# Delta layer: sixteen broadcast transfers issued from ScalarE's queue instead of SyncE's

## The chip, the cores and the metric

The kernel runs on one core of one Trainium2 chip. The metric is the device time of one execution in microseconds (us), median of three runs. Engines are named as the profile names them: PE (TensorE), DVE (VectorE), ACT (ScalarE), POOL (GpSimd), SP (SyncE, here only a queue from which transfers are issued).

## What is computed

One inference step of a two-layer decoder trunk, for 512 prompt positions and 8 sample rows together (520 columns), model width 1024. Layer 0 mixes tokens by causal pooling, layer 1 by a gated delta rule with 8 heads of 128; a gated feed-forward layer follows each. The part that the change touches is the delta rule, cut to what matters:

```python
gc = jnp.cumsum(g, axis=-1)                                   # log decay within a chunk
decay = jnp.exp(jnp.where(incl, gc[..., :, None] - gc[..., None, :], -jnp.inf))
a_mat = jnp.where(strict, einsum('id,jd->ij', kb, k) * decay, 0.0) + eye
rhs = jnp.concatenate([vb, kb * jnp.exp(gc)[..., None]], axis=-1)
sol = triangular_solve(a_mat, rhs, lower=True, unit_diagonal=True)
qk = einsum('id,jd->ij', q, k) * decay
q_dec = q * jnp.exp(gc)[..., None]
# then a scan over the chunks with the state S
```

The kernel uses four chunks of 128 positions a head (the result is the same for any chunk length). For `decay` it needs, for each head, `gc` of the chunk's positions as a row that is the same on all 128 partitions; for `q_dec` it needs `exp(gc)` in the same form. Both are made by writing a 32x128 tile to DRAM (`gdr` for gc, `edr` for exp(gc)) and reading it back with every partition getting the same row.

## The kernel before, in words

All arrays are feature-major: 128 partitions hold features, the free axis holds the 520 columns. Every dense product is done as three fp32r matmuls (high times high, high times low, low times high part). The weights stream through as chunks of 128x1024 (512 KB): SP issues the load of `wr` (two buffers), ACT casts it to `wh`, DVE subtracts to get `wl` (class `Weights`, lines 312 to 368). A new load is issued only when `wl` has been made from the buffer that it overwrites (`adv_lo`, line 351).

The delta layer's input product runs tile by tile (32 tiles of 128 output features; each takes two halves of 24 matmuls on PE). Around it, for each of eight heads, a set of small tasks is put in between: `t_em` (decay of a pair of heads, line 1136), `t_head` (transposes, norms, products of keys and queries, line 1151), `t_v`, `t_leaf` and `levels` (triangular inverse, on POOL and PE), `t_scan` and `t_out` (state scan), `t_norm`, `t_split`, and `t_sample` for the sample rows.

The order is made when the program is built. A planner (`Clock`, `Engine`, `Background`, lines 48 to 309) keeps an expected time for each engine and for each buffer, and lays down a task's next instructions when the expected time of PE has reached the time at which their inputs are expected. Each engine then executes its own list strictly in the order in which it was laid down, whatever the real times are; PE too. So an instruction laid down too early makes its engine stand, with all that is behind it. For a transfer the planner expects this (lines 166 to 172):

```python
if op == "dma_start":
    t = max([self.c.at.get(name, 0.0), self.c.dma[0]] + [...ready...])
    self.c.dma[0] = t + 0.48
    self.c.dma[1] = max(t + 1.1, self.c.dma[1]) + 4 * outs[0].shape[0] * n / 3.6e5
    self.c.at[name] = t
    cost = 0.06
    extra = self.c.dma[1] + 0.9 - t
```

`name` is the issuing engine, so `self.c.at[name] = t` sets the expected time of that engine to the time of the issue. With both inputs ready and no earlier transfer under way, a 128x512 tile is expected 1.1 + 0.73 + 0.9 = 2.73 us after its issue.

The two transfers in question:

- `em[h]` <- `gdr` (line 1142, in `t_em`): 128x512 f32, 256 KB, for both heads of a pair one after the other. DVE then makes four pieces per head (`em<-em,lg,msk`, line 1146), ACT the exponential (line 1133), and DVE uses it in `U` (line 1194) and in `em<-em,pk` (line 1197).
- `vn[h]` <- `edr` (line 1181, in `t_head`): the same size, one per head. DVE multiplies the queries with it (`kq<-kq,vn`, line 1202). That buffer later holds the values (`t_v`, line 1219), so the tile has two uses.

Eight of each: 16 transfers, 4 MB. Besides these SP issues all weight loads, the small stores of states, and the spills. ACT issues eight loads of `in_ssm` (line 1474) in the delta layer.

The sample task of a pair (`t_sample`, line 1466) makes two small products on DVE (`s_sq`, `s_pr`, lines 1482 and 1483) and lays a small PE matmul group behind them (`p_q<-ones,s_sq`, line 1486).

In the text, em(h) and vn(h) are the transfers of head h, counted from 0.

Of the kernel before, what the change touches and what calls it, by code (L numbers as in the profile page):

```python
# [22 lines left out]
NH, NCH = 8, 4  # L23
# [363 lines left out]
def _emit(tc, nc, clk, E, P, a, o):  # L387
    V, S, G, PE, SP = (E[k] for k in ("DVE", "ACT", "POOL", "PE", "SP"))
# [20 lines left out]
    def aux(name="aux"):  # L409
        k = min((k for k in banks if banks[k] is None), key=bank_at)  # L410
        banks[k] = (psd["p"] if k == "r3" else psa).tile([128, 512], F32, name, tag=k, bufs=1)[:]
        return banks[k]

    def give(p):
        k, = (k for k in banks if banks[k] is p)
        banks[k] = None
# [534 lines left out]
    def delta_in(res, dp, oz, oz1, r8):  # L951
# [11 lines left out]
        gdr = dram.tile([32, 128], F32, "gdr")  # L963
        edr = dram.tile([32, 128], F32, "edr")
# [45 lines left out]
        def t_ab():  # L1010
# [60 lines left out]
            SP.dma_start(out=gdr, in_=gcT)  # L1071
            flags.add("gc")
            bg.add(t_em(0), 0)
            yield [lg[:]], "ACT", None
            S.activation(out=eg, in_=lg, func=AF.Exp)
# [35 lines left out]
        em, kq, U, kd, vn, vt, v, vf = {}, {}, {}, {}, {}, {}, {}, {}  # L1111
# [7 lines left out]
        def alloc(kind, shape=(128, NCH, 128)):  # L1119
            return dp.tile(list(shape), F32, kind, bufs=bufs[kind])  # L1120

        def take(kind, n=1):
            assert free[kind] >= n
            free[kind] -= n
# [5 lines left out]
        def em_exp(hh):  # L1130
            act_table("exp_and_others")
            for h in hh:
                S.activation(out=em[h], in_=em[h], func=AF.Exp)
                done["em"].add(h)

        def t_em(pair):
            hh = (2 * pair, 2 * pair + 1)
            yield [gdr[:], lambda: dp.free_at("em", bufs["em"])], None, both(lambda: "gc" in flags, can("em", 2))
            take("em", 2)
            for h in hh:  # L1140
                em[h] = alloc("em")
                SP.dma_start(out=em[h], in_=gdr[:].rearrange("(c h) i -> h c i", h=8)[h].unsqueeze(0).broadcast_to([128, NCH, 128]))
            for h in hh:
                for c in range(NCH):
                    yield [em[h][:]] if c == 0 else [], "DVE", None
                    V.scalar_tensor_tensor(out=em[h][:, c, :], in0=em[h][:, c, :], scalar=gcl[:, 0, hc(c, h)], in1=msk,
                                           op0=ALU.subtract, op1=ALU.min)
            yield [em[hh[1]][:]], "ACT", lambda: "ln" in flags
            em_exp(hh)

        def t_head(h):
            yield [], None, both(is_done("kq", h), can("kd"), lambda: "eg" in flags)
            take("kd")
            for i in (0, 1):
                yield [kq[h][:, i, :], aux_free], None, aux_ok
                pt = aux("pt")
                for c in range(NCH):
                    PE.transpose(pt[:, tok[c]], kq[h][:, i, tok[c]], ident)
                n2 = dp.tile([128, NCH], F32, "n2", bufs=4)
                if i == 0:  # L1160
                    kd[h] = alloc("kd")
                for c in range(NCH):
                    yield [pt[:, tok[c]]], "ACT", None
                    jk = dp.tile([128, 128], F32, "jk")
                    S.activation(out=jk, in_=pt[:, tok[c]], func=AF.Square, accum_out=n2[:, c:c + 1])
                    if i == 0:
                        S.activation(out=kd[h][:, c, :], in_=pt[:, tok[c]], func=AF.Copy, scale=ekd[:, hc(c, h)])
                give(pt)
                yield [n2[:]], "DVE", None
                if i == 0:  # L1170
                    V.tensor_scalar(out=n2, in0=n2, scalar1=EPS, scalar2=None, op0=ALU.add)
                    bg.add(t_nk(h, n2), 2)
                    r = dp.tile([128, NCH], F32, "n2r", bufs=2)
                    V.reciprocal(out=r, in_=n2)
                    V.tensor_tensor(out=sc_s[:, h, :], in0=r, in1=beta[:, 0:4, h], op=ALU.mult)
                else:
                    V.tensor_scalar(out=epsq[:, h, :], in0=n2, scalar1=EPS, scalar2=EPS * 128.0, op0=ALU.add, op1=ALU.mult)
            yield [edr[:]], None, both(lambda: "er" in flags, can("vn"))
            take("vn")
            vn[h] = alloc("vn")  # L1180
            SP.dma_start(out=vn[h], in_=edr[:].rearrange("(c h) i -> h c i", h=8)[h].unsqueeze(0).broadcast_to([128, NCH, 128]))
            yield [], None, both(is_done("em", h), can("U"))
            take("U")
            U[h] = alloc("U")
            for c2 in range(2):
                yield [kq[h][:], aux_free], None, aux_ok
                pk = aux("pk")
                for q in range(2):
                    c = 2 * c2 + q
                    PE.matmul(pk[:, q * 256:q * 256 + 256], kq[h][:, 0, tok[c]], kq[h][:, :, tok[c]], start=True, stop=True)  # L1190
                for q in range(2):
                    c = 2 * c2 + q
                    yield [pk[:, q * 256:q * 256 + 256], em[h][:, c, :], sc_s[:, h, :]], "DVE", None
                    V.scalar_tensor_tensor(out=U[h][:, c, :], in0=pk[:, q * 256:q * 256 + 128], scalar=sc_s[:, h, c:c + 1],
                                           in1=em[h][:, c, :], op0=ALU.mult, op1=ALU.mult)
                yield [], "DVE", None
                V.tensor_tensor(out=em[h][:, 2 * c2:2 * c2 + 2, :], in0=em[h][:, 2 * c2:2 * c2 + 2, :],
                                in1=pk[:].rearrange("p (q x) -> p q x", q=2)[:, :, 128:], op=ALU.mult)
                give(pk)

            yield [vn[h][:]], "DVE", None
            V.tensor_tensor(out=kq[h][:, 1, 0:T], in0=kq[h][:, 1, 0:T], in1=vn[h][:].rearrange("p c x -> p (c x)"), op=ALU.mult)
            done["head"].add(h)

        def t_nk(h, n2):
            yield [n2[:]], "POOL", None
            G.tensor_tensor(out=nk[:, h, :], in0=n2, in1=half[:, 0:NCH], op=ALU.pow)
            done["nk"].add(h)
# [436 lines left out]
        for pair in range(NH // 2):  # L1645
            hh = (2 * pair, 2 * pair + 1)
            if pair:
                bg.add(t_em(pair), PE_)
            bg.add(t_leaf(pair), PL)
            bg.add(t_sample(pair), 0.55)  # L1650
            for h in hh:
                bg.add(t_head(h), PH)
                bg.add(t_v(h), 5)
                bg.add(t_scan(h), PS)
                main_take("kq")
                kq[h] = alloc("kq", (128, 2, NT))
                def fin(i, h=h):
                    G.tensor_copy(ksm[:, h, i, :], kq[h][:, i, T:])
                    if i:
                        done["kq"].add(h)  # L1660
                        done["ks"].add(h)
                tile_(8 + h, kq[h][:, 0, :], lambda h=h, f=fin: f(0, h))
                tile_(h, kq[h][:, 1, :], lambda h=h, f=fin: f(1, h))
# [138 lines left out]
```

## Time and profile before

| what | value |
|---|---|
| median of 3 runs | 1145.2 us (1145.11 to 1146.39) |
| the profiled execution's own time | 1146.64 us |
| its span, first to last instruction | 1144.7 us |
| mean granted clock of PE over the span | 0.995 |
| delta layer in the span | from about 410 to 720 us |
| PE / DVE / ACT / POOL busy over the span | 99% / 69% / 46% / 30% |
| weight loads (512 KB each), median from issue to landing | 3.4 to 3.6 us |
| em<-gdr, vn<-edr (256 KB each), median from issue to landing | 5.0 us, 5.9 us |
| s_ub<-udr (256 KB, the same kind, in the last feed-forward layer) | 4.1 us |

How to read it: the span is one execution, measured by the hardware profiler; the execution's own time has 1.9 us around it. A share of busy time is an average over all stages. "Idle before, releaser" in a timeline is how long an engine stood before an instruction and what let it go on. In a timeline the second column is the length of a merged run of instructions, and "x4" the number merged. "issue" is time in which an engine waited for nothing that the profile shows. PEclk 1.00 is the upper of TensorE's two clock levels (2.4 GHz), 0.50 the lower (1.2 GHz).

### The profile page before, as it was taken

The numbers are of one execution on the slowest core, as the hardware profiler recorded it, in microseconds if no ns is written. First come the engines' busy times: TensorE is split into PE (matmuls) and PEld (weight loads), VectorE is DVE, ScalarE is ACT, GpSimd is POOL, SyncE is SP. The second block draws the span as 40 slices with busy tenths as digits, with TensorE's granted clock in tenths as the row PEclk, the third lists the DMA queues.
The fourth block names the chain that finished last, engine by engine and source line by source line (L and its number), as shares of the span: only waits on it lengthen the run. The fifth ranks groups of instructions, "written<-read, shape, count | busy, mean of one in ns | idle before, by whom it ended". The sixth has DMA issues, their size and how long they took to land.

```text
span 1144.7 us, 23401 instructions
## 1 busy us (share of the span) xinstructions
PE 1129.7 (99%) x9544; PEld 1108.8 (97%) x9544; DVE 787.6 (69%) x1448; ACT 523.7 (46%) x969; POOL 349.0 (30%) x520
## 2 busy tenths in 40 slices
PE   9999999999999999999999999999999999999996
PEld 8999999999999999999989998999999999999996
DVE  6877777777443358887788765569998989752224
ACT  5544444444322238757675745544444444432222
POOL 4212111111000021376537560424545445201010
PEclk9999999999999999999999999999999999999999
DMA  8232322232433333432333323244544554343322
GB/s 293 76 110 86 100 85 101 85 99 82 134 105 104 107 120 119 110 97 85 90 121 89 102 62 122 74 142 148 148 148 148 142 153 137 120 116 96 92 84 75
DMA packets 71069, 128.96 MB, mean 113 GB/s; under 512 B 5324, under 2 KB 42700, under 8 KB 70963
## 3 DMA queue, kind: packets, MB, share of 16 engines
q1 hardware_dynamic: 61667, 122.22, 34.9%
q10 hardware_dynamic: 9296, 5.26, 1.6%
q8 instruction: 75, 1.23, 0.4%
q14 instruction: 31, 0.25, 0.1%
HBM read 116.72 MB, written 10.74 MB: 111 GB/s over the span
## 4 chain that ended last, share of the span: by engine, by line
PE 91%; DVE 3%; DMA 2%; ACT 2%; issue 1%; SPq 0%; ACTq 0%; DVEq 0%; POOL 0%
PE ps L151 81%; PE ps_d L151 3%; PE p_s L151 2%; PE p L151 1%; PE po L151 1%; PE pt L151 1%; PE p_q L151 1%; PE pk L151 1%; DVE wl L151 1%; DMA vn<-edr 1%; DVE c L151 1%; DMA em<-gdr 0%; ACT wh L151 0%; DVE x L151 0%; DMA wr<-in_dn_in 0%
## 5 line engine op out<-in xcount | busy, mean ns | idle before, releaser
L151 PE MATMUL ps<-xl,wh 128*128 128x256 f32 (+2 forms) x1936 | 551.1, 285 | 0.0
L151 PE MATMUL ps<-xh,wh 128*128 128x256 f32 (+2 forms) x1936 | 549.3, 284 | 0.0
L151 PE MATMUL ps<-xh,wl 128*128 128x264 f32 (+1 forms) x1920 | 547.1, 285 | 0.1
L151 PEld LDWEIGHTS ps<-xl,wh 128*128 128x128 f32 (+1 forms) x1936 | 363.8, 188 | 1.6 <-issue 0.8
L151 PEld LDWEIGHTS ps<-xh,wl 128*128 128x128 f32 x1920 | 362.5, 189 | 2.1 <-issue 1.2
L151 PEld LDWEIGHTS ps<-xh,wh 128*128 128x128 f32 (+1 forms) x1936 | 363.7, 188 | 0.6
L151 DVE TENSOR_TENSOR wl<-wr,wh 128x1024 fp32r<-128x1024 f32 (+1 forms) x175 | 225.0, 1286 | 104.1 <-ACT wh L151 103.8
L151 ACT CAST wh<-wr 128x1024 fp32r<-128x1024 f32 (+1 forms) x177 | 180.6, 1021 | 201.6 <-PE ps L151 163.9
L151 DVE SCALAR_TENSOR_TENSOR c<-hb,vec,c 128x512 f32<-128x512 f32 x248 | 208.9, 842 | 6.2 <-ACT c L151 2.0
L151 POOL COPY fo<-hb 128x10 f32<-128x10 f32 x88 | 72.3, 822 | 358.0 <-DVE hb L151 344.0
L151 PE MATMUL ps<-gl,wh 128*128 128x256 f32 (+1 forms) x616 | 174.5, 283 | 0.0
L151 PE MATMUL ps<-gh,wl 128*128 128x256 f32 (+1 forms) x616 | 174.0, 283 | 0.0
L151 PE MATMUL ps<-gh,wh 128*128 128x256 f32 (+1 forms) x616 | 173.8, 282 | 0.0
L151 DVE TENSOR_TENSOR hb<-ps,rstd 128x520 f32<-128x520 f32 (+2 forms) x152 | 88.3, 582 | 86.7 <-PE ps L151 86.1
L151 ACT ACTIVATE c<-hb,vec 128x520 f32<-128x520 f32 x112 | 89.9, 804 | 83.4 <-DVE hb L151 82.0
L151 PEld LDWEIGHTS ps<-gh,wh 128*128 128x128 f32 x616 | 116.3, 189 | 0.0
L151 PEld LDWEIGHTS ps<-gl,wh 128*128 128x128 f32 x616 | 115.9, 188 | 0.0
L151 PEld LDWEIGHTS ps<-gh,wl 128*128 128x128 f32 x616 | 115.7, 188 | 0.0
L151 POOL TENSOR_TENSOR acc<-acc,sq 128x520 f32<-128x520 f32 (+2 forms) x30 | 40.2, 1342 | 237.4 <-ACT sq L151 237.4
L151 ACT CAST gh<-c 128x520 fp32r<-128x520 f32 x44 | 27.6, 627 | 99.2 <-DVE c L151 99.2
L151 ACT ACTIVATE sg<-c 128x520 f32<-128x520 f32 x44 | 28.1, 640 | 96.7 <-DVE c L151 96.7
L151 POOL TENSOR_TENSOR lt<-lL,lx 128x60 f32<-128x60 f32 (+24 forms) x124 | 51.1, 412 | 23.8 <-DVE s_sq L151 10.1
(268 smaller groups left out, 1359.6 us busy)
## 6 DMA issues: line engine op xcount, KB each, us to landing
wr<-in_up SPq DMA_DIRECT2D x88, 512.0 KB, 3.5
wr<-in_dn_in SPq DMA_DIRECT2D x32, 512.0 KB, 3.6
wr<-in_down SPq DMA_DIRECT2D x32, 448.0 KB, 3.4
wr<-in_down SPq DMA_DIRECT2D x16, 512.0 KB, 3.5
s<-in_ssm ACTq DMA_DIRECT2D x8, 512.0 KB, 4.5
wr<-in_dn_out SPq DMA_DIRECT2D x8, 512.0 KB, 3.5
s<-in_ssm SPq DMA_DIRECT2D x16, 256.0 KB, 3.8
s_ub<-udr SPq DMA_DIRECT2D x16, 256.0 KB, 4.1
```

Of the source, the lines that this page charges most:

```text
L151: r = f(*a, **k)
```

## The change

Both `dma_start` calls are made on ACT's queue (`S`) in place of SP's (`SP`). Nothing else is changed in the source; since the planner is told of the engine that issues, it may lay down the instructions behind it in another order.

```diff
@@ t_em
             for h in hh:
                 em[h] = alloc("em")
-                SP.dma_start(out=em[h], in_=gdr[:].rearrange("(c h) i -> h c i", h=8)[h].unsqueeze(0).broadcast_to([128, NCH, 128]))
+                S.dma_start(out=em[h], in_=gdr[:].rearrange("(c h) i -> h c i", h=8)[h].unsqueeze(0).broadcast_to([128, NCH, 128]))
@@ t_head
             vn[h] = alloc("vn")
-            SP.dma_start(out=vn[h], in_=edr[:].rearrange("(c h) i -> h c i", h=8)[h].unsqueeze(0).broadcast_to([128, NCH, 128]))
+            S.dma_start(out=vn[h], in_=edr[:].rearrange("(c h) i -> h c i", h=8)[h].unsqueeze(0).broadcast_to([128, NCH, 128]))
```

## Rows read from the trace of the kernel before

**Rows 1.** The page, section 1: busy time and share of each engine.
```profile
PE 1129.7 (99%) x9544; PEld 1108.8 (97%) x9544; DVE 787.6 (69%) x1448; ACT 523.7 (46%) x969; POOL 349.0 (30%) x520
```

**Rows 2.** Busy time by stretch: length, PE, PEld, DVE, ACT, POOL, PEclk, DMA share, GB/s.
```profile
410.00:480.00 70.00, 68.35 (x546) 66.98 (x545) 57.58 (x146) 48.79 (x103) 16.64 (x29) 0.98 0.45 130
480.00:700.00 220.00, 219.68 (x2104) 206.63 (x2103) 164.10 (x428) 139.99 (x408) 126.86 (x301) 1.00 0.31 92
700.00:720.00 20.00, 18.16 (x150) 17.41 (x149) 10.92 (x26) 10.14 (x30) 2.06 (x3) 1.00 0.28 100
```

**Rows 3.** PE's timeline at 472 to 479 us, and one row at 714 us.
```profile
474.25 0.20 PE L151 MATMUL p_q<-ones,s_sq 128*32 128x1 f32 x2 [1.65 <-DVE s_pr L151]
...
474.62 0.39 PE L151 MATMUL ps<-xl,wh 128*128 128x256 f32 x1
...
478.22 0.29 PE L151 MATMUL ps<-xh,wl 128*128 128x256 f32 x1
...
478.83 0.28 PE L151 MATMUL ps<-xh,wh 128*128 128x256 f32 x1
...
714.23 0.39 PE L151 MATMUL ps<-oh,wl 128*128 128x256 f32 x1 [0.92 <-ACT oh L151]
```

**Rows 4.** The chain of waits at 460 to 474 us: start, length, what.
```profile
460.95 1.23 DVE wl L151
...
462.58 6.22 DMA vn<-edr
...
473.96 0.15 DVE s_sq L151
```

**Rows 5.** DVE's timeline, 462 to 507 us.
```profile
462.89 0.34 DVE L151 SCALAR_TENSOR_TENSOR em<-em,lg,msk 128x128 f32<-128x128 f32 x1
...
466.10 0.87 DVE L151 SCALAR_TENSOR_TENSOR em<-em,lg,msk 128x128 f32<-128x128 f32 x3
468.82 0.69 DVE L151 TENSOR_TENSOR kq<-kq,vn 128x512 f32<-128x512 f32 x1 [1.85 <-DMA vn<-edr]
...
506.32 0.69 DVE L151 TENSOR_TENSOR kq<-kq,vn 128x512 f32<-128x512 f32 x1
```

**Rows 6.** SP's timeline, 437 to 502 us (issues of transfers).
```profile
437.36 0.93 SPq L151 DMA_DIRECT2D em<-gdr  x2
...
455.83 0.93 SPq L151 DMA_DIRECT2D em<-gdr  x2
462.19 0.35 SPq L151 DMA_DIRECT2D wr<-in_dn_in  x1
462.58 0.44 SPq L151 DMA_DIRECT2D vn<-edr  x1
...
501.03 1.07 SPq L151 DMA_DIRECT2D vn<-edr  x1
```

**Rows 7.** ACT's timeline, 437 to 503 us.
```profile
437.12 1.28 ACT L151 ACT_TABLE_LOAD   x1
...
459.41 1.09 ACT L151 CAST wh<-wr 128x1024 fp32r<-128x1024 f32 x1
...
461.87 0.72 ACT L151 ACTIVATE c<-hb,vec 128x520 f32<-128x520 f32 x1
...
469.65 1.05 ACT L151 CAST wh<-wr 128x1024 fp32r<-128x1024 f32 x1
469.81 0.40 ACTq L151 DMA_DIRECT2D s<-in_ssm  x1
470.72 1.28 ACT L476 ACT_TABLE_LOAD   x1
...
502.77 0.28 ACT L151 ACTIVATE jk<-pt 128x128 f32<-128x128 f32 x1
```

**Rows 8.** The tiles em, then vn: their transfers, from issue to landing.
```profile
DMA to landing us min/median/max: 4.5/5.0/6.3
...
DMA to landing us min/median/max: 5.3/5.9/6.4
```

## The prediction

> **What bounds the kernel now.** I read the page's busy times first: PE is busy for 99% of the span [rows 1], so a change elsewhere can only win time in which PE stands or runs slowly. Then the busy time by stretch of the delta layer, the only stage with these transfers: PE is busy 68.35 of 70 us, 219.68 of 220 and 18.16 of 20 [rows 2]. It stands for 1.65 + 0.32 + 1.84 = 3.8 us in 310, and the granted clock is below 1.00 in the first stretch alone. PE's timeline shows where: before 474.25 it stands 1.65 us at a `p_q` matmul whose inputs DVE had not made, and after that the clock is at the lower level: 17 matmul steps from 474.62 to 478.22 take 3.60 us, 0.212 each, while the five to 478.83 take 0.122 each [rows 3]. The slow stretch so costs 3.60 - 17 x 0.122 = 1.5 us. Around 712 to 715, where the last heads end, PE stands three times, for at most 0.92 us, and the clock stays at 1.00 [rows 2, 3].
>
> Then the chain of waits for the first gap: DVE makes a `wl` at 460.95; the weight load of that buffer and then vn(1) leave SP behind it at 462.58; the transfer takes 6.22 us; `s_sq`, which the PE matmul needs, comes only at 473.96 [rows 4]. DVE's timeline says what that cost: DVE ends the em pieces of the second pair at 466.10 + 0.87 = 466.97 and waits 1.85 us for vn(1) [rows 5]. Without that wait PE's would be about gone. So the most that the change can win here is 1.65 + 1.5 = 3.2 us, and 1.8 more at the layer's end if it also made the last heads earlier, for which I see no reason: their chain runs through POOL's triangular steps, whose input is the product U and not vn.
>
> All rows are from one execution, of 1146.64 us with a span of 1144.7; the median of the runs is 1145.2, 1.4 lower. I work out differences in the span and take them from the median. A measurement of this kernel can tell about 0.2% from no change, 2.3 us.
>
> **The issue, step by step.** Sixteen issues leave SP and enter ACT's list. SP's list holds transfers only, so SP runs ahead: it issues what the planner laid down as soon as the buffer or the weight before it allows. ACT's list holds casts and activations, and an issue there goes when ACT gets to it. Where it would stand is read off from the order in which the code before lays its instructions down:
> - em(0), em(1): SP issues them at 437.36, right after `gdr` has landed [rows 6]. ACT has a table load at 437.12 before them [rows 7] and would have to stand for the same landing: no gain. ACT stands at most some 0.3 us, plus the issues.
> - em(2), em(3): SP at 455.83 [rows 6]; in ACT's list behind the cast at 459.41 [rows 7], so 459.6: 3.8 us later.
> - vn(1), the one that matters: SP at 462.58 behind the weight load of 462.19 [rows 6]; in ACT's list behind the activation `c` of 461.87 [rows 7], so 462.0: 0.6 us earlier.
> - vn(3): SP at 501.03 [rows 6]; behind ACT's square at 502.77 [rows 7], so 502.9: 1.9 us later.
>
> So "not behind weight loads" holds for vn(1), but not in general.
>
> **What each is worth.** Landing: em takes 4.5 to 6.3 us from its issue, 5.0 in the middle; vn takes 5.3 to 6.4 [rows 8], the same bytes but mostly right behind a weight load.
> 1. em(2) issued at 459.6 lands at 464.1 (4.5), 464.6 (5.0) or at the latest 465.9 (6.3). DVE now begins its first piece at 462.89 [rows 5]: a new DVE wait of 1.2 to 3.0 us. I take the middle landing, 1.7.
> 2. vn(1) issued at 462.0 lands at 467.3 (5.3) to 468.4 (6.4). I use the vn range and not em's 4.5, since the weight load of 462.19 is in flight in either case, and em(2), em(3) now stand right ahead of it. DVE, pushed to 466.97 + 1.7 = 468.7 by the first wait, no longer waits for it.
> 3. So DVE loses 1.7 us in place of 1.85: a gain of 0.2, rounded up; with the ends, from 1.2 (gain 0.6) to 3.0 (loss 1.2). PE's gap is then about 1.5 us. That is nearer to the 1.65 that was followed by the lower clock than to the 0.92 that was not [rows 3], so I keep the slow stretch at 1.5.
> 4. vn(3) lands at 502.9 + 5.3 to 6.4 = 508.2 to 509.3; DVE wants it at 506.32 [rows 5]: a wait of 1.9 to 3.0 us that isn't there now. What hides it: PE's dense product writes three PSUM regions in turn, each half tile takes 24 matmuls x 0.122 = 2.9 us, so an eviction on DVE may be 5.8 us late before PE stands. Cost 0. If a small PE matmul is laid close behind DVE there, it costs what the wait is, up to 3.0, and a slow stretch of 1.5.
> 5. ACT's time for 16 issues: a load of `in_ssm` was issued at 469.81 for 0.40 us inside the cast of 469.65 to 470.70, and the next instruction began at 470.72 [rows 7]. Cost 0; the upper bound, were none hidden, is 16 x 0.44 [rows 6] = 7 us of ACT, spread over some 200 us of a stretch in which ACT is busy 64% [rows 2], so still not PE's.
> 6. SP without them: the weight loads come no earlier, since they wait for DVE's `wl` (462.19 is the end of the one of 460.95 [rows 4, 6]). Gain 0.
>
> Sum: -0.2 us, **1145.0**. By the widest ends of 1 to 3, with all else at 0, it is 1144.6 to 1146.4.
>
> On the queue itself: vn took 5.3 at the least behind a weight load, em 4.5 at the least [rows 8]; taken alone, these two rows say that leaving the weight load's queue wins 0.8 us of landing. The Trainium skill (DMA: Bandwidth & Descriptors, "Issuing engines are not separate DMA queues") speaks against that: transfers issued from different engines run on the same DMA engines and interleave, so another issuing engine saves issue time only. By that rule vn(1) would land its 0.6 us earlier and no more, and if nothing else moved the time would be 1144.6; by em's 4.5 it would land at 466.5, before DVE wants it, and the result would be the first rival below.
>
> **Rivals.**
> A, the gap closes: the planner is told that em(2) is issued later, and may lay its DVE pieces further back, so that wait 1 falls away. Then DVE waits only for vn(1), 467.3 - 466.97 = 0.3 us at best and 1.0 at 468.0, in place of 1.85; PE's gap is 0.1 to 0.8 us, below the 0.92 that left the clock up [rows 3], and the 1.5 is saved too. Gain 0.85 + 1.5 = 2.3 to 1.55 + 1.5 = 3.0: 1142.2 to 1142.9, with 1142.5 in the middle. For it: the planner does see the later issue. Against it: step 3, and that any other order in this stage may open a gap of its own.
>
> B, slower, by consumers laid too early: by its constants the planner expects a 256 KB tile 2.73 us after the issue, while the rows say 4.5 to 6.4 [rows 8]. Up to now SP's lead of up to 3.8 us covered the difference. On ACT the lead is gone, and a DVE operation can stand 1.8 to 3.7 us in front of each em pair and vn, with everything behind it in DVE's list. Where a small PE matmul (`p_q`, `p_s`) is laid within that time behind it, PE stands as well: one more gap like the first, 1.65 + 1.5 = 3.2 us, gives 1148.4. It decides from a gap of about 1 us on; below that the loss stays within what can be told. For it: DVE has waits for these transfers even with the lead (1.85 us [rows 5]), and it is busy 58 of 70 us in the first stretch [rows 2]. Against it: with all of DVE's present waits PE stands for only 3.8 us in 310 [rows 2].
>
> **Chances.** Forecast, a small shift with the gap still there: 0.42, from 1143 to 1147.4. A: 0.29. B: 0.29. A is over 0.2% faster, B over 0.2% slower, the forecast within. The range takes A whole and B to a little over its one gap: 1141.8 to 1148.8.
>
> **What would show it.** Right: em(2) issued near 459.6 and vn(1) near 462.0 on ACT's queue; a DVE wait for em<-gdr near 463 in place of the one for vn; a PE gap of 1.2 to 1.9 us before a `p_q` near 474 with a slow stretch behind it; ACT with no time lost at its issues. Wrong: landings of em and vn much under 4.5 us (A), or the granted clock at 1.00 all through 470 to 480; new PE gaps elsewhere between 440 and 700, or a second stretch below 1.00 (B); a changed gap at the end of the layer, which I hold to be untouched.

## The result, and the profile after

The changed kernel takes 1154.86 us (median of six executions, 1152.35 to 1157.67) against 1146.37 for the kernel before, run on the same chip: ratio 1.0077, 95% interval 1.0064 to 1.009. The forecast was 1145.0, 0.2 less than before, with a range up to 1148.8, so both the number and the sign of the likeliest case were wrong. Ratios here and below are those on record, up to 0.0005 away from the quotient of the medians, and of fast executions alone: one of e1's five, of 2825.47 us, is in neither its ratio nor its median. The profiled execution took 1152.66 us with a span of 1150.7; it is 6.0 longer than the one of before, and the account below is made of those 6.0. The other 2.5 of the difference of the medians has no profile.

Busy time by stretch of the changed kernel (columns as in [rows 2], which its first three lines answer):

```profile
410.00:480.00 70.00, 69.70 (x565) 67.94 (x564) 58.73 (x148) 50.26 (x109) 18.71 (x33) 1.00 0.42 132
480.00:700.00 220.00, 215.61 (x2053) 201.89 (x2053) 162.14 (x424) 134.74 (x389) 123.11 (x297) 0.99 0.30 88
700.00:720.00 20.00, 16.81 (x138) 15.79 (x136) 9.28 (x22) 9.95 (x36) 1.98 (x2) 0.99 0.37 133
...
610.00:620.00 10.00, 6.95 (x49) 6.50 (x48) 8.31 (x19) 6.13 (x7) 6.37 (x15) 0.86 0.29 106
```

The first stretch is now as rival A had it: PE stands 0.30 us in place of 1.65, and the clock is 1.00. The loss is in the other two, where PE stands 4.4 and 3.2 us in place of 0.3 and 1.8. The timeline of PE says where; here are all the rows with a wait of 0.35 us or more, and behind the first the first and the last of its slow steps (a step is the time from one matmul's start to the next one's):

```profile
617.75 0.59 PE L151 MATMUL ps<-xh,wl 128*128 128x264 f32 x1 [3.05 <-DVE hb L151]
618.14 0.42 PE L151 MATMUL ps<-xl,wh 128*128 128x264 f32 x1
...
620.56 0.30 PE L151 MATMUL ps<-xh,wl 128*128 128x264 f32 x1
...
699.69 0.68 PE L151 MATMUL p<-vt,wy 64*64 64x64 f32 x8 [0.68 <-ACT vt L151]
...
714.61 0.63 PE L151 MATMUL pt<-ident,ot 128*128 128x128 f32 x4 [0.38 <-DVE ot L151]
...
716.77 0.63 PE L151 MATMUL pt<-ident,ot 128*128 128x128 f32 x4 [1.53 <-ACT oh L151]
...
718.90 0.39 PE L151 MATMUL ps<-oh,wl 128*128 128x256 f32 x1 [0.92 <-ACT oh L151]
719.63 0.58 PE L151 MATMUL ps<-ol,wh 128*128 128x256 f32 x1 [0.35 <-DVE ol L151]
```

From 618.14 to 620.56 eleven steps take 0.22 us each, where [rows 3] has 0.122: the lower clock (PEclk 0.86 at 610 to 620 above). The chain of waits of the changed kernel around that gap (start, length, what) shows what PE waited for:

```profile
611.89 1.06 ACT wh L151
...
612.98 1.23 DVE wl L151
614.20 1.48 DVE em L151 x4
615.68 0.78 DVE c L151
...
616.49 0.83 DVE c L151 x2
617.32 0.39 DVE hb L151
...
617.75 4.19 PE ps L151 x22
```

The `hb` eviction frees the PSUM region that PE's next tile needs, and it stands in DVE's list behind the em pieces of the last pair and two `c` products. DVE's timeline of the changed kernel at that place, and then that of the kernel before:

```profile
608.77 1.21 DVE L151 TENSOR_TENSOR wl<-wr,wh 128x1024 fp32r<-128x1024 f32 x1
611.45 0.28 DVE L151 COPY s_ur<-p_q 16x128 f32<-16x128 f32 x1 [1.47 <-PE p_q L151]
611.66 0.14 DVE L151 TENSOR_SCALAR s_r<-p_q 16x1 f32<-16x1 f32 x1
611.72 1.11 DVE L151 SCALAR_TENSOR_TENSOR em<-em,lg,msk 128x128 f32<-128x128 f32 x4
612.98 1.23 DVE L151 TENSOR_TENSOR wl<-wr,wh 128x1024 fp32r<-128x1024 f32 x1
614.12 1.56 DVE L151 SCALAR_TENSOR_TENSOR em<-em,lg,msk 128x128 f32<-128x128 f32 x4
...
617.27 0.76 DVE L151 TENSOR_TENSOR hb<-ps,rstd 128x256 f32<-128x256 f32 x2
```

```profile
613.45 0.43 DVE L151 TENSOR_TENSOR hb<-ps,rstd 128x264 f32<-128x264 f32 x1
614.88 0.35 DVE L151 SCALAR_TENSOR_TENSOR em<-em,lg,msk 128x128 f32<-128x128 f32 x1 [1.00 <-DMA em<-gdr]
...
618.11 0.41 DVE L151 TENSOR_TENSOR hb<-ps,rstd 128x256 f32<-128x256 f32 x1
618.44 0.48 DVE L151 SCALAR_TENSOR_TENSOR em<-em,lg,msk 128x128 f32<-128x128 f32 x1
...
619.29 1.46 DVE L151 SCALAR_TENSOR_TENSOR em<-em,lg,msk 128x128 f32<-128x128 f32 x4
```

Nothing on DVE waits for a transfer there after the change: the em pieces run back to back, in two blocks of four, and they hold up the eviction because they are laid ahead of it. Before, the pieces stood between the evictions. The pieces take 1.11 + 1.56 = 2.7 us, and DVE also stands 1.47 us for `p_q` ahead of them, so they are not all of the delay that PE sees as 3.05. It is the order of DVE's list that is new, and not a late DMA. The waits of DVE for the transfers even fell, from 3.1 and 2.8 us in all for em and vn to these (view of the waits, DVE, 430 to 745 us: us in total, times, longest):

```profile
DVE em L151 <- DMA em<-gdr: 2.1, 2, 1.9
DVE kq L151 <- DMA vn<-edr: 0.9, 2, 0.8
```

The account, against the profiled execution of before, over 410 to 740 us:
- PE stands 330 - 322.13 = 7.87 us in place of 330 - 326.19 = 3.81 (busy time in one stretch of 330 us): 4.1 lost. In that are the 1.65 gap gone, 3.05 new at 617, and 2.0 more at the layer's end (0.68, 0.38, 1.53, 0.92 and 0.35, 3.86 in place of 1.84). The rest is in gaps of less than 0.35.
- The lower clock, counted as in the prediction: the 1.5 of [rows 3] is gone. New are 2.42 - 11 x 0.122 = 1.1 after the gap at 617, and 2.82 - 13 x 0.122 = 1.2 behind 720 us, where 13 steps from 720.01 to 722.83 take 0.217 each. Net 0.8 lost.

That is 4.9 of the 6.0; the other 1.1 is not traced.

### The profile page after: what moved, and what is told of

It reads as the page before. It is cut to its first block, busy times and chain, and to the rows that moved or that the text cites. A ratio compares the mean times of both kernels' runs of the same rounds, so it can differ in the third digit from the quotient of the medians.

```text
span 1150.7 us, 23399 instructions
## 1 busy us (share of the span) xinstructions
PE 1130.7 (98%) x9544; PEld 1108.7 (96%) x9544; DVE 788.9 (69%) x1450; ACT 523.1 (45%) x969; POOL 349.0 (30%) x520
## 4 chain that ended last, share of the span: by engine, by line
PE 54%; DVE 2%; ACT 1%; POOL 1%; issue 1%; DMA 1%; DVEq 0%; ACTq 0%; POOLq 0%
PE ps L151 46%; PE p_s L151 2%; PE ps_d L151 1%; PE p L151 1%; PE po L151 1%; PE p_q L151 1%; PE pt L151 1%; PE pk L151 1%; POOL lx L151 1%; DMA vn<-edr 1%; POOL lt L151 0%; ACT oh L151 0%; DVE c L151 0%; ACT uc L151 0%; DVE x L151 0%
## 5 line engine op out<-in xcount | busy, mean ns | idle before, releaser
L151 POOL TENSOR_TENSOR lx<-lx,lt 128x60 f32<-128x60 f32 (+24 forms) x124 | 55.2, 445 | 9.7
```

Of the source, the lines that this page charges most:

```text
L151: r = f(*a, **k)
```

## The experiments

Two things change at once: the queue, and the order of the lists, since the planner is told of the engine that issues. O stands for the theory that the new order costs the time, Q for the theory that ACT's queue costs it. A helper takes them apart: it tells the planner of one engine and issues on the other. The edits are shown against the changed kernel, with the source of each transfer cut to `gdr...` and `edr...`.

**e1: the order of the kernel before, the issues on ACT**

```diff
+        def planned(told, queue, **k):
+            queue.raw.dma_start(**k)
+            told._note("dma_start", (), k)
-                S.dma_start(out=em[h], in_=gdr...)
+                planned(SP, S, out=em[h], in_=gdr...)
-            S.dma_start(out=vn[h], in_=edr...)
+            planned(SP, S, out=vn[h], in_=edr...)
```

> All sixteen transfers are issued from ACT's queue, but the planner is told SP, so that every engine's list of instructions is the one of the kernel before, with the sixteen issues put into ACT's list where they fall. Theory O (the loss comes from another order that the planner laid down): 1143 to 1147 us, no PE gap near 617, PE's gap before p_q near 474 under 1.65 us or gone. Theory Q (the loss comes from ACT's queue itself, by standing at issues or by later or slower transfers): 1152 to 1156, with ACT or DVE waiting over 5 us more than before for em, vn or the issues.

**e2: the order of the changed kernel, the issues on SP**, with the helper of e1

```diff
-                S.dma_start(out=em[h], in_=gdr...)
+                planned(S, SP, out=em[h], in_=gdr...)
-            S.dma_start(out=vn[h], in_=edr...)
+            planned(S, SP, out=vn[h], in_=edr...)
```

> The mirror: the planner is told ACT, so that the order is the one of the changed kernel, but all sixteen transfers are issued from SP. Theory O: 1151 to 1157 us, with the PE gap of about 3 us near 617 and the longer gaps at the layer's end. Theory Q: 1144 to 1148 and neither.

**e3: em alone on ACT**, planner and queue in agreement

```diff
-            S.dma_start(out=vn[h], in_=edr...)
+            SP.dma_start(out=vn[h], in_=edr...)
```

> Only em<-gdr moves to ACT (eight transfers), vn<-edr stays on SP. The order that the planner lays down changes throughout from the first em on. Theory O: it lands anywhere that a new order leads, more likely slower: 1147 to 1157 us. Theory Q: half of the sixteen issues, so about half of the loss: 1148 to 1152.

**e4: vn alone on ACT**, planner and queue in agreement

```diff
-                S.dma_start(out=em[h], in_=gdr...)
+                SP.dma_start(out=em[h], in_=gdr...)
```

> Only vn<-edr moves to ACT, em<-gdr stays on SP. The lists of PE, DVE and POOL are those of the kernel before, instruction by instruction; ACT's differ by the eight issues alone. Theory O: 1142 to 1146 us, since vn(1) is issued up to 0.6 us earlier and not behind the weight load, and PE's gap near 474 shrinks. Theory Q: about half of the loss, 1148 to 1152.

Measured, all four beside the same runs of the kernel before (1146.08 us):

| kernel | order | queue | us | ratio | interval |
|---|---|---|---|---|---|
| e1 | before | ACT | 1151.28 | 1.0046 | 1.0032 to 1.006 |
| e2 | after | SP | 1153.88 | 1.0063 | 1.0049 to 1.0077 |
| e3 | a third one | em on ACT | 1148.15 | 1.0017 | 1.0008 to 1.0026 |
| e4 | before, but for the place of ACT's issues | vn on ACT | 1145.06 | 0.9992 | 0.9983 to 1.0001 |

e2 has none of the sixteen on ACT's queue and still loses nearly all that the change loses (1.0063 beside 1.0077). PE's waits in e2 (us in total, times, longest) are those of the changed kernel, but for one of 0.8 at a `p_q` that waits for a transfer of `in_ssm`; the two longest:

```profile
PE ps L151 <- DVE hb L151: 3.4, 2, 3.2
PE pt L151 <- ACT oh L151: 1.5, 1, 1.5
```

So O holds for the change itself. But Q is no idle theory: e1, with PE's, DVE's and POOL's lists as before, loses 1.0046. Its profiled execution is 5.1 us longer than the one of before, and 3.18 of standing with 1.3 of slow steps behind it are at one place, where the kernel before and the changed one lose nothing. e1's DVE timeline there, then its PE timeline:

```profile
557.24 0.69 DVE L151 SCALAR_TENSOR_TENSOR em<-em,lg,msk 128x128 f32<-128x128 f32 x2 [3.70 <-DMA em<-gdr]
...
559.98 0.67 DVE L151 TENSOR_TENSOR ot<-ot,ms 128x512 f32<-128x512 f32 x1
```

```profile
560.80 0.78 PE L151 MATMUL pt<-ident,ot 128*128 128x128 f32 x4 [3.18 <-DVE ot L151]
```

ACT issues em(4) at 551.85, in its turn behind a row of activations; SP, which runs ahead, had issued it at 547.63. DVE's piece starts 5.39 us after the issue, and DVE stands 3.70 in front of it; in the kernel before it ran at 552.37 without a wait. `ot` behind it is late, and PE with it. This is the mechanism of rival B, in a kernel that keeps the order. In the changed kernel em(4) leaves ACT at 545.59, and no DVE step stands there; it has the `hb` gap instead. So the losses of e1 and of the changed kernel come from different gaps.

e3 and e4 take one kind each. vn alone changes no order but for ACT's own list and costs nothing. em alone makes a third order and costs 1.0017, with a gap of 1.73 at 556.71, where DVE has stood 3.16 for em(4), and one of 1.47 at an `hb` at 618.38. The loss of the whole change comes only with both kinds.

**e5: all on SP, the planner told SP's landing, but its time of ACT moved on to the issue; e6: all on SP, the planner told of ACT's issue and landing, but its time of ACT left alone.** The two halves of what the planner learns from the change.

```diff
 e5
+        def planned(queue, **k):
+            queue.raw.dma_start(**k)
+            SP._note("dma_start", (), k)
+            clk.at["ACT"] = max(clk.at["ACT"], clk.dma[0] - 0.48)
 e6
+        def planned(queue, **k):
+            queue.raw.dma_start(**k)
+            act = clk.at["ACT"]
+            S._note("dma_start", (), k)
+            clk.at["ACT"] = act
 both
+                planned(SP, out=em[h], in_=gdr...)
+            planned(SP, out=vn[h], in_=edr...)
```

> All sixteen transfers stay on SP. Of the two things that the planner reckons differently once it is told that ACT issues them, this run keeps one: its reckoned time of ACT moves on to each issue; the landing is reckoned as of SP. The lists are those of before up to about 600 us; from there PE's list differs. In the lists of the changed kernel the last pair's em pieces stand in two blocks of four ahead of both hb evictions; in this run's lists they stand singly, with an hb eviction between them, as in the kernel before. Theory 1, the loss is the hb gap (3.05 us and its slow stretch of 1.5) and the rest of the lateness at the layer's end comes from it: no gap near 617, the layer's end as before, 1145 to 1147 us, ratio 0.999 to 1.002. Theory 2, any new order makes the last heads late, hb gap or not: no gap near 617, but PE waits at the layer's end of 3 us or more in place of 1.84, some of it with the lower clock, 1148 to 1151, ratio 1.002 to 1.005. Theory 3, ACT's reckoned time is what makes the hb gap: the gap of 3 us is back near 617, 1152 to 1155.

> The other half: all sixteen transfers stay on SP, the planner reckons their issue and landing as if ACT issued them, and its reckoned time of ACT is left as it was. The lists are those of before up to about 490 us and differ from there. The em pieces of the last pair stand singly between hb evictions. Theory 1 (the hb gap is the loss): no gap near 617, 1145 to 1147 us, ratio 0.999 to 1.002. Theory 2 (the last heads come late in any new order): PE waits at the layer's end of 3 us or more in place of 1.84, 1148 to 1152, ratio 1.002 to 1.006. Theory 3 (the later landing is what makes the hb gap): a gap of 3 us near 617, 1152 to 1155.

**e7: the changed kernel, the last pair's em pieces given a lower standing**

```diff
-                bg.add(t_em(pair), PE_)
+                bg.add(t_em(pair), 3 if pair == 3 else PE_)
```

> The changed kernel, its issues on ACT, with the last pair's em pieces given a lower standing in the planner, so that DVE makes them behind the c and hb work; order as in the changed kernel up to about 611 us. If the hb gap with its slow stretch is all of the loss that can be had back (theory 1): no PE gap near 617, the layer's end as in the changed kernel, 1154.9 - 4.6 = 1150.3, ratio 1.004. If those pieces feed the last heads and DVE has no room for them later (theory 2): no gap near 617, but the last heads later than in the changed kernel by some us, PE waits at the layer's end of 6 us or more in place of 3.5, 1155 to 1162, ratio 1.008 to 1.014.

Measured beside 1146.0 for the kernel before: e5 1151.71 (ratio 1.0047, 1.0032 to 1.0062), e6 1152.85 (1.0057, 1.0042 to 1.0072), e7 1160.24 (1.012, 1.0103 to 1.0137). In none of the three does PE wait for an `hb` for more than 0.2 us near 617. The busy times by stretch, first of e5 from 600 on, then of e6 and of e7 from 700 on, and last of e3 for comparison (columns as in [rows 2]):

```profile
600.00:700.00 100.00, 99.40 (x970) 94.37 (x971) 69.97 (x185) 56.84 (x158) 54.52 (x132) 1.00 0.31 90
700.00:740.00 40.00, 35.28 (x263) 33.97 (x263) 20.98 (x43) 19.78 (x54) 9.33 (x9) 0.87 0.25 84
```
```profile
700.00:740.00 40.00, 34.80 (x252) 32.89 (x251) 20.77 (x43) 20.78 (x58) 8.59 (x8) 0.87 0.23 72
```
```profile
700.00:740.00 40.00, 31.86 (x258) 28.88 (x259) 17.01 (x38) 20.13 (x59) 5.64 (x6) 0.83 0.17 58
```
```profile
700.00:740.00 40.00, 39.60 (x327) 38.80 (x326) 24.81 (x47) 22.64 (x50) 11.04 (x10) 1.00 0.33 114
```

PE stands 4.7, 5.2 and 8.1 us behind 700 where before it stood 1.84, with a lower clock between. Theory 1 of these runs, that the `hb` gap is the loss, falls: without that gap the time is still 1.0047 to 1.012. Theory 2 holds for these three orders: in each the last heads end later, when PE's dense work has run out and nothing covers them (e5 and e6 came 0.7 and 0.85 us above the top of the range that it gave in time; e6's time lies in theory 3's range, but without theory 3's gap). It does not hold for any new order, as it was worded: in e3's PE stands 0.40 us behind 700, less than before. The chain of the last heads can be followed at one DVE step, the `lvr` transpose behind the last of POOL's triangular steps. Here it is in the kernel before, and then in e5,

```profile
680.46 0.44 DVE L151 STREAM_TRANSPOSE lvr<-lx 128x256 f32<-128x256 f32 x1
```
```profile
684.79 0.43 DVE L151 STREAM_TRANSPOSE lvr<-lx 128x256 f32<-128x256 f32 x1
```

which is 4.3 us later; in e6 it is 4.65 later (685.11), in the changed kernel 5.9 (686.34), in e7 16.1 (696.56), and in e3 1.0 (681.49). The transpose `lL` ahead of POOL's steps, at 648.48 before, is later by 2.2 in e5, 4.4 in e6 and 2.8 in the changed kernel. In e6 nearly all of the lateness is there at `lL`, in front of which DVE stands for ACT's `uc` copies; they begin at 648.16 in place of 643.37:

```profile
652.90 1.25 DVE L151 STREAM_TRANSPOSE lL<-uc 128x1024 f32<-128x1024 f32 x1 [3.57 <-ACT uc L151]
```

In e5 and in the changed kernel it is spread over the steps ahead of `lL` and behind it, and no one wait carries it. Which choice of the planner brings it stays open. Each half of what the planner is told costs most of the loss alone; among the runs with all sixteen, the `hb` gap came only with both halves together.

**e8: e1 with em(4) and em(5) back on SP**; the order of before, fourteen transfers on ACT. **e9: e4 again, with more rounds.**

```diff
 e8, against e1
-                planned(SP, S, out=em[h], in_=gdr...)
+                planned(SP, SP if pair == 2 else S, out=em[h], in_=gdr...)
```

> The order of the kernel before on every engine, fourteen of the sixteen transfers issued on ACT as in e1; only em(4) and em(5) go back to SP. If e1 lost its 5 us at the one place where DVE stood 3.70 us for em(4) (PE's gap of 3.18 us at 560.80 and a slow stretch of about 1.4 behind it): DVE's piece of em(4) waits for nothing, that gap is gone, the gap near 474 stays at about 1.5, ratio 1.0046 less (3.2 + 1.4) / 1146 = 1.0006, between 0.999 and 1.002, 1145 to 1148 us. If the ACT queue costs wherever it is used (in ACT's time, or by many small waits of DVE): the ratio stays at 1.003 or above.

> The kernel of e4 once more, with more rounds: order of the kernel before on PE, DVE and POOL, vn issued on ACT, em on SP. If the 0.9 us that it takes off the gap near 473 counts, alone or with the slow stretch: ratio 0.997 to 0.9992 with an interval under 1. If the time at the layer's end gives it back: 0.9995 to 1.0005.

Measured beside 1145.92: e8 1146.19 (ratio 1.0003, 0.9994 to 1.0012), e9 1144.62 (0.999, 0.9981 to 0.9999). With two of sixteen issues moved back, e1's loss is gone: it was the DVE wait for that pair, and ACT's queue costs nothing elsewhere that can be told. e8's stretches are those of before, the gap near 474 among them:

```profile
410.00:480.00 70.00, 68.55 (x548) 67.26 (x547) 57.43 (x146) 48.87 (x104) 16.10 (x31) 0.98 0.45 130
480.00:600.00 120.00, 119.69 (x1132) 111.70 (x1131) 91.89 (x238) 80.22 (x241) 70.40 (x165) 1.00 0.32 95
```

e9 is the best version measured. vn(1) leaves ACT at 461.49, DVE waits 0.33 us for it in place of 1.85, and the gap at `p_q` is down to 0.29; these rows of its DVE, its ACT and its PE timeline answer [rows 5], [rows 7] and [rows 3]:

```profile
467.46 0.69 DVE L151 TENSOR_TENSOR kq<-kq,vn 128x512 f32<-128x512 f32 x1 [0.33 <-DMA vn<-edr]
```
```profile
461.48 0.28 ACT L151 ACTIVATE jk<-pt 128x128 f32<-128x128 f32 x1
461.49 0.38 ACTq L151 DMA_DIRECT2D vn<-edr  x1
461.65 0.20 ACT L151 ACTIVATION_READ_ACCUMULATOR jk<-pt 128x1 f32 x1
```
```profile
472.90 0.20 PE L151 MATMUL p_q<-ones,s_sq 128*32 128x1 f32 x2 [0.29 <-DVE s_pr L151]
```

The same kernel had 0.9992 in e4 and 0.999 here: about 1 us gained. That is under the 0.2% that the forecast took as its bound, but the two measurements agree and the second interval ends below 1. The half of the change that its name speaks of, vn out from behind a weight load, so does what it says, by an issue 1.1 us earlier; from the issue to the DVE step vn(1) takes 5.97 us, beside 6.24 before.

## Why the prediction was wrong

**The step that failed** is the sentence under "The issue, step by step": "Where it would stand is read off from the order in which the code before lays its instructions down." It gave the right issue times for a kernel that keeps its order, and this one didn't. All six terms of the sum were worked out on DVE's and PE's lists of before, while the planner, by the quoted `self.c.at[name] = t` and the landing reckoned from it, lays down another order from the first em on. e2 shows that this order costs 1.0063 by itself, with the queue unchanged.

**A second step failed beside it.** The steps and the sum take up em(0) to em(3), vn(1) and vn(3), and leave em(4) at nothing without a reason. e1 is the kernel that the sum describes, the order of before with all sixteen on ACT, and it takes 1151.28, above the range: em(4) leaves 4.2 us later than from SP, and its DVE wait of 3.70 costs PE 3.18 and a slow stretch of 1.3. So the forecast would have missed with the order kept, too.

Point by point:
- **Issue times.** In e1, where the order is kept, ACT issues em(2) at 459.59, vn(1) at 462.29, vn(3) at 503.19; forecast were 459.6, 462.0 and 502.9. In the changed kernel em(2) leaves at 459.61 too, but vn(1) at 460.70 and vn(3) at 500.53, since the list is another.
- **Steps 1 to 3**, em(2) late and vn(1) earlier: in e8, which keeps the order, DVE waits 0.60 us for em(2) and 0.82 for vn(1), together 1.42, in place of 1.85; forecast was 1.7 for em(2) and none for vn(1). PE's gap there is 1.45 with the slow stretch behind it (forecast 1.5), and the time is 1146.19 beside 1145.92, a change of +0.3 (forecast -0.2). The two terms missed in opposite directions and about cancelled, so that the near hit is partly luck; and this kernel, with em(4) and em(5) left on SP, is not the one that was asked about.
- **In the changed kernel** DVE waits 0.21 us for em(2), none for vn(1), and the gap at `p_q` is gone with its slow stretch: what rival A described. In that stretch 1.35 of standing and the 1.5 were won, 2.9 us, within A's 2.3 to 3.0. "Any other order in this stage may open a gap of its own" stood among the reasons against A, without a place and without a price. It was the main effect.
- **Rival B** had the right sign, and in e1 the right mechanism, at too low a price: 3.2 for a gap with its slow stretch, where e1 has 3.18 + 1.3 = 4.5. In the change DVE stands less for the transfers than before, so B is not why it is slower.
- **Step 5** held for PE, and for ACT in part. ACT is busy 523.1 us in place of 523.7, and a single issue of 0.38 us lies beside a 0.28 us activation and the one behind it with no time lost (e9's ACT rows above). But behind the second of two issues in a row ACT can stand, as at em(5) in e1, where in the kernel before the same copy runs without a wait; PE shows none for it:
```profile
552.25 0.52 ACTq L1110 DMA_DIRECT2D em<-gdr  x1
552.82 0.27 ACT L151 COPY ot<-po 128x128 f32<-128x128 f32 x1 [0.61 <-issue]
```
- **Step 6** held: in e8 the weight load beside vn(1) leaves SP at 462.44, in the kernel before at 462.19 [rows 6].
- **Step 4** held for vn(3): DVE waits 0.18 us for it near 505 in the changed kernel and 1.01 in e8 (forecast 1.9 to 3.0), and PE doesn't. But its bound, an eviction 5.8 us late before PE stands, is what the new order broke at 617: PE's last matmul of the half tile that the `hb` at 617.27 frees ends at 608.49, and the eviction comes 8.8 us behind it.
- **"For which I see no reason"**, on the last heads: wrong. Their chain doesn't wait for vn, but its steps stand in lists that the new order changes. 2.0 us more of PE's standing and 1.2 of lower clock are at the layer's end, outside the stretch on which the argument was built.

**On the queue.** The Trainium skill (DMA: Bandwidth & Descriptors, "Issuing engines are not separate DMA queues") says that transfers issued by different engines run on the same DMA engines, so that another issuing engine saves only the time that it takes to initiate the transfer. In e4 and e9, with em on SP, vn on ACT and the order kept, the median landing of vn is 6.0 us, beside the 5.9 of [rows 8]: no gain in the middle from leaving the weight loads' queue, as the page has it (the shortest is 4.4 in place of 5.3). With the other order the median is 4.8 in the changed kernel and 5.6 in e2, whose sixteen are on SP:

```profile
DMA to landing us min/median/max: 4.4/4.8/8.5
```
```profile
DMA to landing us min/median/max: 4.8/5.6/8.8
```

In the changed kernel em is on ACT as well as vn, and the transfers start at other moments than in e2; which of these makes the 0.8 us wasn't tried, and the page's rule doesn't give it. In e8 vn(1), the one that mattered, took 6.88 us from its issue at 461.86 to the DVE step at 468.74, which had stood 0.82 us for it: no less than the 6.22 before [rows 4].

## What to carry to other kernels

Where a planner writes the order, moving an issue to another engine is two changes, the queue and the order, and the second can be the larger: compare the lists first, and separate the two by telling the planner one thing and doing the other. A transfer that moves from a queue that runs ahead to an engine's own list loses its lead, so move only those whose consumer waits now (here vn), and leave those that the lead covers (here em(4) and em(5)). Where PE is busy for 99%, a new order can win little and lose more: give it a price of its own, from the gaps that such orders show, and look at the stage's end too, where nothing is left to cover a late chain.

## What was not expected of the hardware

The granted clock after a gap isn't settled by the length of that gap. Before the same `p_q` near 474 a gap of 1.65 us [rows 3], and ones of 1.46 in e1 and 1.45 in e8, were followed by some 17 matmul steps at 0.21 us; in e5 a gap of 1.88 was followed by none. At the `hb` near 617 the gap of 3.05 in the changed kernel was followed by eleven slow steps, and the gap of 3.23 in e2 by none. The busy time of PE at 470 to 480 us in e8 and then in e5, and at 610 to 620 us in e2, beside the 0.86 of the changed kernel:

```profile
470.00:480.00 10.00, 8.55 (x60) 8.36 (x59) 9.61 (x20) 7.61 (x10) 5.44 (x11) 0.83 0.53 153
```
```profile
470.00:480.00 10.00, 8.12 (x70) 7.93 (x69) 9.83 (x19) 7.93 (x13) 5.55 (x9) 1.00 0.51 150
```
```profile
610.00:620.00 10.00, 6.77 (x56) 6.33 (x55) 9.00 (x21) 6.14 (x7) 5.48 (x14) 1.00 0.34 106
```

The same at the layer's end: PE stands 1.84 us behind 700 in the kernel before, in e4 and in e9, with a clock of 1.00 there in the first and the last, and 0.91 at 700 to 720 in e4. So the 1.5 us that the prediction put down to the slow stretch as a fixed price is in some executions and not in others.
